# Up projection of a hybrid decoder block: a place in the ring and a pass order for each of twenty units, and a four-column fp32 product in every granule

## The chip, the cores and the metric

The kernel runs on one core of a Trainium2 chip. Its time is the device time of one execution in microseconds. TensorE (PE) multiplies, with weight loads (PEld) that can run ahead of the products; VectorE (DVE), ScalarE (ACT) and GpSimd (POOL) work beside it, and SyncE (SP) issues most transfers. Each engine works off its own queue in order.

## The reference

One decoder layer on x of 512 tokens by 2048 features, all in float32:

```python
def conv_ffn(h, w_ffn_in, conv_w, conv_b, w_ffn_out):
    S = h.shape[1]
    up = h @ w_ffn_in                       # 512 x 2048 by 2048 x 11264
    a, b = up[..., :D_FF], up[..., D_FF:]   # D_FF = 5632
    a_pad = jnp.pad(a, ((0, 0), (CONV_W - 1, 0), (0, 0)))
    a = (conv_w[0] * a_pad[:, 0:S] + conv_w[1] * a_pad[:, 1:S + 1]
         + conv_w[2] * a_pad[:, 2:S + 2] + conv_b)
    return (jax.nn.gelu(a, approximate=True) * b) @ w_ffn_out

def reference(x, ...):
    h = rmsnorm(x, attn_pre_norm)
    m = token_mixer(h, ...)       # gated linear attention and differential attention, then w_o
    x = x + rmsnorm(m, attn_post_norm)
    h = rmsnorm(x, ffn_pre_norm)
    f = conv_ffn(h, w_ffn_in, conv_w, conv_b, w_ffn_out)
    return x + rmsnorm(f, ffn_post_norm)
```

The change lies in the product `h @ w_ffn_in`, called the up projection.

## The kernel before

**Split products.** A float32 product is made from three products in the reduced format fp32r. Each operand v is split into a high half (v rounded to fp32r, by ACT, line 135) and a low half (v minus the high half, by DVE, line 136); then w·s is taken as high·high, high·low and low·high. The activations are split once and stay: `ah` and `al` hold them transposed. The weights come from memory in granules of 128 partitions by 1,024 values and are split on the way.

**The ring.** The two halves of a granule go to `ring`, one tile of 7 × 1,024 values for each partition. There are three slots for high halves (0, 1, 2) and three for low halves (3, 4, 5), and the seventh thousand is room behind them. `halves` steps the slot by one, modulo three, and returns the high and the low range; both are moved up by `place_w[0]` elements, which is the *place* of the weights. Before the change the place is 16 in the up projection's units and 0 everywhere else. One element has four bytes.

**Units.** After the first block of 512 columns, done plainly, the up projection is cut into 20 units: ten blocks of 512 columns for each of the two branches a and b of the reference. A unit multiplies in Strassen–Winograd form: seven products of blocks (`x0`, `z0`, `y0`, `z1`, `x1`, `y1`, `y2`) with the activation sums `a11`, `a12`, `a22`, `s5`, `s2`, `s3`, `s7`, and weight sums that are made in place, by accumulating transfers that POOL issues (line 873) and by DVE. `Unit.run` does one such product: two granules, each split by `granule` and multiplied by `up_prods`. There a granule is 4 rows of blocks (k) by 2 column blocks (n) by 3 passes, 24 products of a 128 × 128 weight block with 256 columns of activations (lines 924 to 926): the weights are the stationary operand, so that every product has its own weight load.

**Order.** The loop at the end of the functions shown runs one unit after the other, with the ends laced: `x0` of the next unit comes before `y2` of this one, and `z0` of the next after it. The down projection's units (`a` of 2, products of 512 columns, lines 1021 to 1023) follow in the same manner, the first one's `x0` before the last up unit's `y2`. Chains `x` and `z` accumulate in the PSUM pool `psm`, `y` in the pool `psa`, with four banks each. This stage is not in an order written by hand: the framework's planner orders each engine's instructions with a timeline of its own, and puts in the waits that overlapping reads and writes need.

Of the kernel before, what the change touches and what calls it, by code (L numbers as in the profile page):

```python
# [9 lines left out]
F32 = mybir.dt.float32  # L10
# [20 lines left out]
GR = 1024  # L31
# [4 lines left out]
def hybrid_layer(ctx: ExitStack, tc: tile.TileContext, x, attn_pre_norm, w_in, w_alpha_up, b_alpha,  # L36
# [19 lines left out]
    mm = nc.tensor.matmul  # L56
# [5 lines left out]
    psa = ctx.enter_context(tc.tile_pool(name="psa", bufs=4, space=PSUM))  # L62


    ident = few.tile([P, P], F32, name="ident")
# [11 lines left out]
    def bank(pool=None):  # L77
        return (pool or psa).tile([P, 512], F32, name="bank", tag="bank")
# [27 lines left out]
    place_w = [0]  # L106

    ring = wpool.tile([P, 7 * GR], F32R, name="ring", bufs=1)
    slot = [0]

    def halves():
        slot[0] = (slot[0] + 1) % 3
        return [ring[:, GR * i + place_w[0]:GR * (i + 1) + place_w[0]] for i in (slot[0], slot[0] + 3)]

    kept = []

# [9 lines left out]
    def granule(src, a, raw=None, spare=None, hl=None):  # L126
        if raw is None:
            raw = load(src, a)
        if hl is not None:
            hi, lo = hl[:, 0, :], hl[:, 1, :]  # L130
        elif spare:
            hi, lo = spare_halves(spare)
        else:
            hi, lo = halves()
        act(hi, raw, AF.Copy)  # L135
        tt(lo, raw, hi.bitcast(F32), ALU.subtract)  # L136
        r = "p (a b) -> p a b"
        return hi.rearrange(r, a=a), lo.rearrange(r, a=a)
# [8 lines left out]
    def split(hi, lo, src):  # L147
        act(hi, src, AF.Copy)  # L148
        tt(lo, src, hi.bitcast(F32), ALU.subtract)  # L149
# [485 lines left out]
    order = [(s + 8) % 16 for s in range(KT)]  # L635
# [129 lines left out]
    def pair_tile():  # L765
        return small_tile("u").rearrange("p (n t) -> p n t", n=2)


    def conv(c, b, f):
        act(c, b, AF.Identity, bias=conv_col(3, f), scale=conv_col(2, f))  # L770
        stt(c[:, 1:], b[:, :S - 1], conv_col(1, f), c[:, 1:], ALU.mult, ALU.add)
        stt(c[:, 2:], b[:, :S - 2], conv_col(0, f), c[:, 2:], ALU.mult, ALU.add)
        act(c, c, AF.Gelu_apprx_tanh)
# [27 lines left out]
    HK = KT // 2  # L801
# [50 lines left out]

    turn = [0]
    extra = [False]

    class Unit:
        def __init__(self, a, block, prods, chain, out):
# [3 lines left out]
        def run(self, seg, op, raws):  # L861
            c = seg[0]
            if seg[1] == "0":
                self.banks[c] = self.chain(c)
            for g in range(2):
                turn[0] += 1
                place_w[0] = 16 if self.a == 4 else 0
                hl = granule(None, self.a, raws[g], spare=extra[0] and turn[0] % 4 == 0)
                self.prods(self.banks[c], op, g, hl, seg[1] == "0")

# [42 lines left out]
    NOW = dict(skip_group_check=True)  # L913


    def up_prods(b, op, g, w, start):
        sh, sl = up[op]
        for n in range(2):
            o = b[:, 256 * n:256 * (n + 1)].rearrange("p (t c) -> p t c", c=P)
            for k in range(4):  # L920
                wh = w[0][:, k, n * P:(n + 1) * P]
                wl = w[1][:, k, n * P:(n + 1) * P]
                kk = 4 * g + k
                mm(o, wh, sh[:, :, kk, :], start=start and kk == 0 and n == 0, stop=False, **NOW)  # L924
                mm(o, wh, sl[:, :, kk, :], start=False, stop=False, **NOW)  # L925
                mm(o, wl, sh[:, :, kk, :], start=False, stop=kk == HK - 1, **NOW)  # L926

    held = {}

    def up_unit(gi, br):  # L930
        col0 = DFF * br + 512 * gi
        T = [slice(0, 256), slice(256, 512)]
        st = {}

        def block(i, j, g):
            return w_f3[:, HK * i + 4 * g:HK * i + 4 * g + 4, col0 + 256 * j:col0 + 256 * (j + 1)]

        def chain(c):
            return bank(psa if c == "y" else psm)

        def out(seg, b):
            v = b.rearrange("p (n t) -> p n t", n=2)
            if seg == "x0":
                st["p1"] = fp.tile([P, 2, 256], F32, name="p1", tag="p1", bufs=2)
                act(st["p1"], v, AF.Copy)
            elif seg == "z0":
                st["u1"] = pair_tile()
                tt(st["u1"][:, :, T[1]], v, st["p1"], ALU.subtract)
            elif seg == "y0":
                stt(st["u1"][:, :, T[0]], v, -1.0, st["p1"], ALU.mult, ALU.subtract)  # L950
            elif seg == "z1":
                tt(st["u1"][:, :, T[0]], st["u1"][:, :, T[0]], v, ALU.add)
            elif seg == "x1":
                st["u0"] = pair_tile()
                act(st["u0"][:, :, T[0]], v, AF.Copy)
            elif seg == "y1":
                tt(st["u1"][:, :, T[1]], st["u1"][:, :, T[1]], v, ALU.subtract)
                if br == 0:
                    activate(1)
                else:  # L960
                    product(1)
            elif seg == "y2":
                tt(st["u0"][:, :, T[1]], v, st["p1"], ALU.add)
                if br == 0:
                    activate(0)
                else:
                    product(0)
                    token_sums(gi, st["u0"], st["u1"])

        def activate(j):  # L970
            c = held[gi, j] = pair_tile()
            for n in range(2):
                conv(c[:, n, :], st[f"u{j}"][:, n, :], 4 * gi + 2 * j + n)

        def product(j):
            u = st[f"u{j}"]
            tt(u, u, held.pop((gi, j)), ALU.mult)

        return Unit(4, block, up_prods, chain, out)


    def token_sums(gi, u0, u1):
        c, i = (gi - 1) // 2, (gi - 1) % 2
        T = [slice(0, 256), slice(256, 512)]
        a11, a21, a12, a22 = u0[:, :, T[0]], u0[:, :, T[1]], u1[:, :, T[0]], u1[:, :, T[1]]

        def put(n, src):
            dma(sd[c][n][:, i, :].rearrange("p (n t) -> p n t", n=2), src)

        def add(n, x, y, op):  # L990
            t = fp.tile([P, 2, 256], F32, name=n, tag="sum", bufs=2)
            tt(t, x, y, op)
            put(n, t)
            return t

        put("a11", a11)
        put("a12", a12)
        put("a22", a22)
        s5 = add("s5", a21, a22, ALU.subtract)
        s2 = add("s2", s5, a11, ALU.subtract)  # L1000
        add("s7", a11, a21, ALU.subtract)
        add("s3", s2, a12, ALU.add)
# [4 lines left out]
    def piece(v, t, h):  # L1007
        return v[:, t, HK * h:HK * (h + 1), :].rearrange("p k c -> p (k c)")

    def prepare(c, n):  # L1010
        raw = small_tile("st")
        dma(raw, sd[c][n].rearrange("p g x -> p (g x)"))
        split(piece(ah, *place[n]), piece(al, *place[n]), raw)
# [17 lines left out]
    def down_unit(c, cb):  # L1031
# [17 lines left out]

        return Unit(2, block, down_prods, chain, out)  # L1050

    ups = [up_unit(gi, br) for gi in range(1, NG) for br in range(2)]
    for i, u in enumerate(ups):
        nxt = ups[i + 1] if i + 1 < len(ups) else None
        if i == 0:
            u.x0()
            u.z0()
        u.y0()
        u.z1()
        if i == 0:  # L1060
            for h, r in enumerate(s7raw):
                split(up["s7"][0][:, h], up["s7"][1][:, h], r)
        if nxt is None:
            prepare(0, "a11")
        u.x1()
        if nxt is None:
            prepare(0, "s5")
        u.y1()
        if nxt is not None:
            nxt.x0()  # L1070
            u.y2()
            nxt.z0()
        else:
            downs = [down_unit(c, cb) for c in range(NG // 2) for cb in range(2)]
            downs[0].x0()
            prepare(0, "s2")
            u.y2()
# [125 lines left out]
    for q, at in enumerate(((3, 1), (0, 0))):  # L1203
        raw = small_tile("st")
        dma(raw, ud0[:, 2 * q:2 * q + 2, :].rearrange("p n t -> p (n t)"))
        hi, lo = (piece(v, *at) for v in (ah, al))
# [34 lines left out]
```

## Time and profile before

| what | us |
|---|---|
| two runs | 2150.64 and 2164.94, median 2157.79 |
| span of the profiled execution | 2150.8 |
| PE busy | 2112.4 |
| DVE busy | 1414.6 |
| ACT busy | 898.3 |
| up projection's units, first to last product | 928 to 1706 |

The profiled execution's own time is not given apart from its span; the span agrees with the lower of the two runs to 0.2 us. Where a start is given it counts from the first instruction. The duration of a product in the trace (276 ns for 256 columns) has the time through the array in it, and products overlap: how fast they follow each other is seen from their starts, or from how many lie in a stretch of time. A plain fp32 product shows as two instructions, each with a weight load; an fp32r product or a transpose shows as one.

### The profile page before, as it was taken

The page shows a single profiled execution, that of the slowest core. Times are in us where ns is not written, and L with a number is a line of the kernel's source. Part 1 is how long each engine was busy: PE and PEld are TensorE (multiplying, and loading weights), DVE is VectorE, ACT ScalarE, POOL GpSimd, SP SyncE. Part 2 cuts the span into 40 slices and gives each one's busy share as a digit, 9 for nine tenths or more (in the row PEclk, how much of TensorE's full clock was granted, in tenths as well). Part 3 has the DMA queues.
Part 4 walks back from the last instruction along what each step waited for, and adds up shares of the span by engine and source line. Part 5 has one row for each costly group of instructions (what it writes and reads, how often), then busy time and mean ns, then how long its engine had stood idle before and what let it go on. Part 6 is the DMA issues. An engine that isn't in the chain of part 4 may idle for free.

```text
span 2150.8 us, 31861 instructions
## 1 busy us (share of the span) xinstructions
PE 2112.4 (98%) x13009; PEld 1875.4 (87%) x13009; DVE 1414.6 (66%) x1725; ACT 898.3 (42%) x1162; POOL 199.2 (9%) x242
## 2 busy tenths in 40 slices
PE   7999999999999999999999999999999899999998
PEld 6878888888888889999999999999999778787786
DVE  5345554443444237688777786777778777888887
ACT  4233332333343224344544553544454554443433
POOL 1000000000000001011111111111110111110100
PEclk9999999999999999999999999999999999999999
DMA  6322222223224335455776757667577777676653
GB/s 214 99 75 79 79 69 79 79 79 88 78 80 169 95 128 186 128 119 136 172 172 149 175 139 189 149 157 191 129 172 177 203 229 182 171 195 170 158 167 145
DMA packets 218471, 303.83 MB, mean 141 GB/s; under 512 B 11776, under 2 KB 155572, under 8 KB 216404
## 3 DMA queue, kind: packets, MB, share of 16 engines
q1 hardware_dynamic: 165204, 238.87, 33.4%
q0 software_dynamic: 53120, 62.92, 19.1%
q8 instruction: 102, 1.67, 0.3%
q14 instruction: 45, 0.37, 0.1%
HBM read 273.97 MB, written 27.79 MB: 140 GB/s over the span
## 4 chain that ended last, share of the span: by engine, by line
PE 46%; issue 45%; POOL 4%; DVE 3%; DMA 2%; ACT 1%; POOLq 0%; SPq 0%; DVEq 0%; ACTq 0%
PE bank L189 7%; PE bank L190 7%; PE bank L191 7%; PE bank L173 5%; PE bank L171 5%; PE bank L172 5%; POOL rt L873 2%; PE bank L926 2%; PE bank L925 2%; PE bank L924 2%; POOL raw L873 2%; PE bank L439 1%; PE bank L507 1%; PE bank L538 1%; DVE ring L136 1%
## 5 line engine op out<-in xcount | busy, mean ns | idle before, releaser
L136 DVE TENSOR_TENSOR ring<-raw,ring 128x1024 fp32r<-128x1024 f32 x305 | 371.6, 1221 | 353.8 <-ACT ring L135 344.1
L135 ACT ACTIVATE ring<-raw 128x1024 fp32r<-128x1024 f32 x305 | 323.1, 1060 | 596.6 <-PE bank L191 157.3
L926 PE MATMUL bank<-ah,ring 128*128 128x256 f32 x1280 | 353.7, 276 | 0.8 <-DVE ring L136 0.8
L924 PE MATMUL bank<-ah,ring 128*128 128x256 f32 x1280 | 353.5, 276 | 0.0
L925 PE MATMUL bank<-al,ring 128*128 128x256 f32 x1280 | 353.4, 276 | 0.0
L136 DVE TENSOR_TENSOR ring<-rt,ring 128x1024 fp32r<-128x1024 f32 x221 | 269.0, 1220 | 89.8 <-ACT ring L135 87.9
L135 ACT ACTIVATE ring<-rt 128x1024 fp32r<-128x1024 f32 x221 | 233.1, 1060 | 223.5 <-PE bank L925 146.1
L926 PEld LDWEIGHTS bank<-ah,ring 128*128 128x128 f32 x1280 | 240.3, 188 | 1.2 <-DVE ring L136 1.2
L925 PEld LDWEIGHTS bank<-al,ring 128*128 128x128 f32 x1280 | 240.4, 188 | 0.1
L924 PEld LDWEIGHTS bank<-ah,ring 128*128 128x128 f32 x1280 | 240.3, 188 | 0.1
L189 PE MATMUL bank<-ring,ah 128*128 128x512 f32 x600 | 236.9, 398 | 0.8 <-ACT ah L148 0.8
L190 PE MATMUL bank<-ring,ah 128*128 128x512 f32 x600 | 235.8, 394 | 0.0
L191 PE MATMUL bank<-ring,al 128*128 128x512 f32 x600 | 235.0, 394 | 0.0
L171 PE MATMUL bank<-ah,ring 128*128 128x512 f32 (+1 forms) x512 | 196.2, 383 | 0.0
L173 PE MATMUL bank<-ah,ring 128*128 128x512 f32 (+1 forms) x512 | 194.7, 380 | 0.0
L172 PE MATMUL bank<-al,ring 128*128 128x512 f32 (+1 forms) x512 | 194.5, 380 | 0.0
L1022 PE MATMUL bank<-ring,ah 128*128 128x512 f32 x424 | 166.7, 393 | 7.3 <-DVE ring L136 7.2
L1023 PE MATMUL bank<-ring,al 128*128 128x512 f32 x424 | 165.8, 391 | 0.0
L1021 PE MATMUL bank<-ring,ah 128*128 128x512 f32 x424 | 158.8, 393 | 3.2 <-ACT ring L135 2.4
L191 PEld LDWEIGHTS bank<-ring,al 128*128 128x128 f32 x600 | 113.2, 189 | 24.3 <-DVE al L149 0.3
L189 PEld LDWEIGHTS bank<-ring,ah 128*128 128x128 f32 x600 | 113.1, 189 | 24.2 <-ACT ah L148 1.2
L190 PEld LDWEIGHTS bank<-ring,ah 128*128 128x128 f32 x600 | 113.3, 189 | 23.7 <-DVE ring L136 0.5
(260 smaller groups left out, 4063.6 us busy)
## 6 DMA issues: line engine op xcount, KB each, us to landing
raw<-in_w_in_dram SPq DMA_DIRECT2D x96, 512.0 KB, 3.7
raw<-in_w_ffn_in_dram SPq DMA_DIRECT2D x96, 512.0 KB, 5.1
raw<-in_w_ffn_out_dram SPq DMA_DIRECT2D x48, 512.0 KB, 7.3
rt<-in_w_ffn_in_dram SPq DMA_DIRECT2D x40, 512.0 KB, 6.6
rt<-in_w_ffn_in_dram POOLq DMA_DIRECT2D x40, 512.0 KB, 6.2
raw<-in_w_ffn_in_dram POOLq DMA_DIRECT2D x40, 512.0 KB, 6.8
raw<-in_w_o_dram SPq DMA_DIRECT2D x32, 512.0 KB, 3.7
rt<-in_w_ffn_out_dram SPq DMA_DIRECT2D x20, 512.0 KB, 8.1
```

Source lines behind the costliest of these rows:

```text
L135: act(hi, raw, AF.Copy)
L136: tt(lo, raw, hi.bitcast(F32), ALU.subtract)
L171: mm(o, wh, ah[:, t0:t1, kk, :], start=st, stop=False)
L172: mm(o, wh, al[:, t0:t1, kk, :], start=False, stop=False)
L173: mm(o, wl, ah[:, t0:t1, kk, :], start=False, stop=sp)
L189: mm(banks[t], ah[:, t, s, :], w[0][:, k, :], start=st, stop=False)
L190: mm(banks[t], ah[:, t, s, :], w[1][:, k, :], start=False, stop=False)
L191: mm(banks[t], al[:, t, s, :], w[0][:, k, :], start=False, stop=sp)
L924: mm(o, wh, sh[:, :, kk, :], start=start and kk == 0 and n == 0, stop=False, **NOW)
L925: mm(o, wh, sl[:, :, kk, :], start=False, stop=False, **NOW)
L926: mm(o, wl, sh[:, :, kk, :], start=False, stop=kk == HK - 1, **NOW)
L1022: mm(b[j], sh[:, o:o + P], w[1][:, q, :], start=False, stop=False, **NOW)
```

## The change

Each of the 20 units gets a place for its high halves, a place for its low halves, and an order of the three passes: 0 is (high, high), (high, low), (low, high), as before, and 1 is (high, high), (low, high), (high, low). Units of the down projection keep place 0. In every granule of an up unit, ahead of the first product of the second column block, there is one small product in plain fp32: the identity matrix as weights, four columns of the low half as the moving operand, into a PSUM bank of its own, `nudge`, that nothing reads.

```diff
     def halves():
         slot[0] = (slot[0] + 1) % 3
-        return [ring[:, GR * i + place_w[0]:GR * (i + 1) + place_w[0]] for i in (slot[0], slot[0] + 3)]
+        return [ring[:, GR * i + p:GR * (i + 1) + p] for i, p in ((slot[0], place_w[0]), (slot[0] + 3, place_w[-1]))]
...
             for g in range(2):
                 turn[0] += 1
-                place_w[0] = 16 if self.a == 4 else 0
+                place_w[:] = self.places if self.a == 4 else (0,)
+                order[0] = self.order if self.a == 4 else 0
                 hl = granule(None, self.a, raws[g], spare=extra[0] and turn[0] % 4 == 0)
...
                 kk = 4 * g + k
-                mm(o, wh, sh[:, :, kk, :], start=start and kk == 0 and n == 0, stop=False, **NOW)
-                mm(o, wh, sl[:, :, kk, :], start=False, stop=False, **NOW)
-                mm(o, wl, sh[:, :, kk, :], start=False, stop=kk == HK - 1, **NOW)
+                if n == 1 and k == 0:
+                    mm(nudge[0][:, 0:4], ident, wl.bitcast(F32)[:, 0:4], start=True, stop=True, **NOW)
+                passes = [(wh, sh), (wh, sl), (wl, sh)] if order[0] == 0 else [(wh, sh), (wl, sh), (wh, sl)]
+                for i, (w1, s1) in enumerate(passes):
+                    mm(o, w1, s1[:, :, kk, :], start=start and kk == 0 and n == 0 and i == 0,
+                       stop=kk == HK - 1 and i == 2, **NOW)
...
+    nudge = [bank(psa)]
     ups = [up_unit(gi, br) for gi in range(1, NG) for br in range(2)]
+    RELATIONS = [(16, 16, 0), (80, 80, 0), (12, 12, 0), (20, 20, 0), (14, 14, 0), (18, 18, 0), (16, 80, 0), (80, 16, 0),
+                 (16, 0, 0), (16, 32, 0), (16, 16, 1), (80, 80, 1), (12, 12, 1), (20, 20, 1), (16, 48, 1), (88, 88, 0),
+                 (72, 72, 0), (0, 16, 1), (16, 0, 1), (16, 112, 0)]
+    for u, (hi, lo, o) in zip(ups, RELATIONS):
+        u.places, u.order = (hi, lo), o
```

More of the change, by code (lines that the diff above doesn't have):

```diff
@@ L854, in hybrid_layer @@
     extra = [False]
+    order = [0]
     class Unit:
```

## The prediction

> **What bounds the kernel now.** I read the page first, then the table by stage, then the waits inside the up projection, then the order of time around its end.
>
> ```profile
> span 2150.8 us, 31861 instructions
> PE 2112.4 (98%) x13009; PEld 1875.4 (87%) x13009; DVE 1414.6 (66%) x1725; ACT 898.3 (42%) x1162; POOL 199.2 (9%) x242
> PEclk9999999999999999999999999999999999999999
> ```
>
> TensorE is busy 98% of the span at full granted clock; DVE has a third of the span free. Whatever the change adds to the stream of products comes out at the end, unless it fits into a gap, and there are hardly any. Waits of PE, then of ACT, from 925 to 1688 us:
>
> ```profile
> PE bank L926 <- DVE ring L136: 1.8, 4, 0.6
> ACT ring L135 <- PE bank L925: 256.5, 186, 2.8
> ```
>
> In 763 us PE lost 1.8 us to a late split. ACT's waits (total, times, longest) say how the stage runs: the high half of a granule goes into the ring as soon as L925, the last reader of a high half, is done with the slot. That release is for the granule three before, so the split has two granules of PE time in hand. Note that L925 ends it and not L926, which reads only the low half: reuse of the ring is followed by address range within the tile.
>
> How fast PE goes is in the table by stretches (us, PE busy and instructions, PEld, DVE, ACT, POOL, clock, DMA share, GB/s):
>
> ```profile
> 854.00:884.00 30.00, 30.00 (x252) 30.00 (x251) 8.77 (x10) 5.30 (x6) 0.00 (x0) 1.00 0.42 131
> 930.00:940.00 10.00, 10.00 (x87) 10.00 (x86) 9.83 (x9) 5.29 (x7) 0.00 (x0) 1.00 0.33 85
> 950.00:1130.00 180.00, 180.00 (x1591) 180.00 (x1590) 136.44 (x140) 87.31 (x97) 22.90 (x18) 1.00 0.69 164
> 1140.00:1340.00 200.00, 200.00 (x1767) 200.00 (x1766) 150.63 (x153) 91.66 (x99) 26.08 (x21) 1.00 0.72 171
> ```
>
> All four hold products of 256 columns with nothing missing; a count includes up to two products cut by the window's ends. The first (weights at place 0, or in spare tiles) gives 30/250 = 120 ns for a product. The other three have place 16: 10/85 = 118 ns before a short wait near 943 us, and 180/1589 = 113.3 ns after it. So the pace depends on where the weights lie, and at one place it has at least two values, with a short break between them. The change touches just that.
>
> **The parts of the change.** There are 20 units of 7 products of blocks, with 2 granules each: 280 granules of 24 products, 6,720 in all (2,240 of each of the three lines).
>
> ```profile
> L924 PE MATMUL bank<-ah,ring 128*128 128x256 f32 x1280 | 353.5, 276 | 0.0
> L924 PE MATMUL bank<-s3h,ring 128*128 128x256 f32 x320 | 88.4, 276 | 0.0
> ```
>
> (s5h and s2h have 320 each as well.)
>
> *The small product.* 280 times, identity as fp32 weights, four fp32 columns. No fp32 product in the trace is that narrow; the nearest are the 64-column ones of L439:
>
> ```profile
> 160.72 0.39 PE L191 MATMUL bank<-ring,al 128*128 128x512 f32 x1
> 160.94 1.00 PE L439 MATMUL bank<-qe,d 128*128 128x64 f32 x8
> 161.75 0.48 PE L189 MATMUL bank<-ring,ah 128*128 128x512 f32 x1
> 162.07 0.33 PE L439 MATMUL bank<-qe,d 128*128 128x64 f32 x2
> 160.72 1.08 PEld L439 LDWEIGHTS bank<-qe,d 128*128 128x128 f32 x8
> 161.72 0.19 PEld L189 LDWEIGHTS bank<-ring,ah 128*128 128x128 f32 x1
> 161.84 0.54 PEld L439 LDWEIGHTS bank<-qe,d 128*128 128x128 f32 x3
> ```
>
> The source makes four products there and the trace has eight, each with its own load: an fp32 product is two passes. From 160.72 to 162.07 are 1.35 us; the two 512-column products take 0.227 each, so eight passes cost 0.896, or 0.112 each. The loads say why: one follows the other by (161.72 − 160.72 − 0.227)/7 = 0.11 us, though 64 columns would stream sooner. Narrower columns therefore save nothing: two passes, 2 × 0.112 = 0.224 us, and nothing hides them, since the load after the second pass has only four columns to hide under. 280 × 0.224 = **62.7 us**. The low end is from the transposes:
>
> ```profile
> L439 PEld LDWEIGHTS bank<-qe,d x224: 187/192/193, 160.7 to 343.4; 128*128 128x128 f32 x112
> L156 PEld LDWEIGHTS bank<-ident,xt x64: 138/140/230, 9.8 to 51.7; 128*128 128x128 f32 x64
> ```
>
> If loads of this product were as short as those around the identity (140 against 192 ns), a pass would cost 0.060 and all of it 34 us. L439 is nearer, being a plain product, so I take 62.7. A gain from the extra work itself is excluded: PE has no idle time that it could fill. It adds no wait (its operands were waited for by the first half of the granule), and its PSUM bank leaves three for the one `y` chain that a unit holds.
>
> *The places and the ring.* Slots are 1,024 elements apart with no room between, so when the place falls from one granule to the next, the new granule's first elements lie on the last ones of the granule just before, which PE reads last. The split must then wait for the previous granule instead of the third before. Units interleave at their ends (`x0` of the next, `y2` of this one, `z0` of the next), so a change of place is crossed two or three times. I went through the 280 granules with the 20 relations, the slots turning by three from the slot that the overlaps of before imply (another start gives 16 and 26, or 20 and 22, in place of the counts below). With high place above low place, as in (80, 16) and twice (16, 0), a high half in slot 2 also overlaps the low half of slot 0, in every third granule of the unit. Counted: 16 granules whose high half waits for the granule before, 27 whose low half alone does; before the change, 1 and 1, both where the place goes from 16 to 0 at the end of the stage. (Overlaps the other way meet only the first 128 elements of a granule two before, which PE has left by then: nothing.) The first of the two in order of time, PE, then ACT and DVE:
>
> ```profile
> 1705.49 0.28 PE L925 MATMUL bank<-al,ring 128*128 128x256 f32 x1
> 1705.61 0.28 PE L926 MATMUL bank<-ah,ring 128*128 128x256 f32 x1
> 1706.92 0.73 PE L1021 MATMUL bank<-ring,ah 128*128 128x512 f32 x2 [1.03 <-ACT ring L135]
> 1708.35 0.50 PE L1022 MATMUL bank<-ring,ah 128*128 128x512 f32 x1 [0.69 <-DVE ring L136]
> 1708.68 0.40 PE L1023 MATMUL bank<-ring,al 128*128 128x512 f32 x1
> 1708.92 0.40 PE L1021 MATMUL bank<-ring,ah 128*128 128x512 f32 x1
> 1705.81 1.06 ACT L135 ACTIVATE ring<-rt 128x1024 fp32r<-128x1024 f32 x1 [1.77 <-PE bank L925]
> 1707.08 1.21 DVE L136 TENSOR_TENSOR ring<-rt,ring 128x1024 fp32r<-128x1024 f32 x1
> ```
>
> Unhindered, L1021 would start at 1705.73 and the product now at 1708.92 four times 0.227 later, at 1706.64: 2.3 us lost. A low half alone: free 0.04 after L926's end at 1705.89 (as ACT after L925), DVE 1.22, PE 0.06 later at 1707.21, where the third product of an up granule was due at 1705.96, and 0.10 for a load that could not run ahead: 1.35 us. 15 × 2.3 + 26 × 1.35 = 34.5 + 35.1 = **69.6 us**. No cover exists: the wait is for PE's own last product, and both products of a granule pair go to the same bank. Behind the waiting split on DVE's queue stand the evacuations and weight sums, a third of DVE's time being free for them.
>
> *The pace.* Twenty relations, one of which (16, 16, first order) is the old one, each re-entered after 280 breaks. Bounds: 113.3 − 0.112 × 1000 = 1.3 ns less, −9 us, if every product ran at the load cadence; 120 ns, +45 us, if all ran as at place 0. The old place shows both 113 and 118 and the other place 120, so I take the middle, 116.6: 6,720 × 3.3 = **+22 us**.
>
> Sum: 62.7 + 69.6 + 22 = 154. The profiled execution spans 2150.8, as the lower run (2150.64); the median 2157.79 lies 7 above. 2157.8 + 154 = **2312**.
>
> **Rivals.** (1) *Small products nearly free.* At 34 us the time is 2283. The Trainium skill (TensorE: Matmul & The Clock Gate, Back-to-back issue gap) gives 1 to 64 columns a floor of about 25 ns; by that, 560 passes would be 14 us and the sum 2264. The 0.112 of L439's 64 columns disagrees. (2) *Splits queued badly.* The other of the two old overlaps, ACT, DVE, then PE:
>
> ```profile
> 1682.69 1.06 ACT L135 ACTIVATE ring<-rt 128x1024 fp32r<-128x1024 f32 x1 [1.66 <-PE bank L925]
> 1690.91 1.22 DVE L149 TENSOR_TENSOR al<-st,ah 128x1024 fp32r<-128x1024 f32 x1 [3.18 <-ACT ah L148]
> 1692.05 1.22 DVE L136 TENSOR_TENSOR ring<-rt,ring 128x1024 fp32r<-128x1024 f32 x1
> 1693.33 0.50 PE L1022 MATMUL bank<-ring,ah 128*128 128x512 f32 x1 [4.65 <-DVE ring L136]
> ```
>
> Here the planner put a split of reloaded sums ahead of the blocked low half on DVE, and that one waited for its load: 4.65 us instead of 1.35. If half of the 26 went so, 13 × 3.3 = 43 more, 2355; all, 2398. Against it: such reloads come at the end of the stage only. (3) *A better state.* The small product sets the stream to a faster pace. At the load cadence of 112 ns the pace term is −9 instead of +22: 2281. For "no change" it must give back all but 43 of the 132 us of the other terms: 13.3 ns a product, so 100 ns decides; at 97 ns the time is 2157.8 + 132.3 − 109.5 = 2181. For it: the pace has states, and transposes load faster. Against: the load cadence of 112 ns. The Trainium skill (TensorE: Matmul & The Clock Gate, Back-to-back issue gap) has N/2.4 + 2.5, which is an estimate of 109 ns for 256 columns, a pace term of −28 and 2262; no stretch quoted here shows it. (4) *The places cause no waits* (the overlaps are not followed as I read them): 2157.8 + 62.7 + 22 = 2242.
>
> **How the numbers follow.** Forecast 0.60; rival 1 0.11; rival 2 0.15; rival 3 0.10, of which 0.04 under 100 ns; rival 4 0.04. 2% (43 us) is about what a measurement of this kernel tells from no change. Faster 0.01, same 0.04, slower 0.95. The range takes in pace ends of the forecast (2281 to 2335), rival 1 below its 2283 by a faster pace, and rival 2 to beyond half: 2250 to 2370.
>
> **What would show it.** The new line's products: 560 in the profile, each granule's first half to its second 0.22 longer. ACT's high-half splits released by the granule just before, 16 times, and DVE's low halves 27 more. PE's idle time in the stage: from 2 to some 60 us, at unit ends and inside the eighth, ninth and nineteenth units. In windows between breaks: 113 to 120 ns, differing by unit. I am wrong if the small product shows one pass, if idle time stays at a few us, or if a unit runs well off 113 to 120.

## The result, and the profile after

The changed kernel takes 2339.55 us (median of 2 runs, 2335.15 to 2343.95) against 2157.79: a ratio of 1.0837, with a 95% interval of 1.0736 to 1.0937. It is slower, as forecast; 2312 was predicted, 27.5 us too little, and the range, 2250 to 2370, holds the time. The profiled execution took 2335.15, its span is 2333.4, so 1.7 us lie around the span.

The page of the changed kernel, to be held against the lines of before:

```profile
span 2333.4 us, 32952 instructions
PE 2238.3 (96%) x13569; PEld 1993.6 (85%) x13569; DVE 1422.6 (61%) x1725; ACT 903.0 (39%) x1162; POOL 199.5 (9%) x242
```

PE has 560 instructions more, all from the small products; DVE, ACT and POOL do what they did. Of the 182.6 us added to the span 126 are busy PE time, and PE's share falls from 98% to 96%, so there is new idle time as well. The stage itself, from the first up product to the last, in the table by stretches (us, PE, PEld, DVE, ACT, POOL, clock, DMA share, GB/s), before and after:

```profile
928.00:1705.70 777.70, 771.21 (x6745) 768.40 (x6743) 597.82 (x607) 376.14 (x411) 101.70 (x80) 1.00 0.69 163
```

```profile
928.00:1891.00 963.00, 898.88 (x7295) 885.62 (x7294) 603.62 (x607) 378.36 (x411) 101.70 (x80) 0.97 0.57 131
```

Two things stand in the second row that the first has not: 64 us in which PE is not busy (6.5 before), and a granted clock of 0.97. The waits of PE in this stage of the changed kernel (total us, times, longest):

```profile
PE bank L930 <- DVE ring L136: 40.9, 35, 2.2
PE bank L930 <- ACT ring L135: 19.9, 20, 1.2
```

Before it was 1.8 us, from 925 to 1688. The products of all three passes now have one line, L930; the small product's is L927.

From the starts of the products in the two traces I summed the stage product by product, from the first up product to the start of the product after the last one: 766.9 us before, 954.8 after, 188 more. (The rest of the kernel is 5 us shorter, most of it in shorter waits of the down projection behind the stage.) By parts:

| term | forecast | measured |
|---|---|---|
| small products, 280 | 62.7 | 63 (0.225 each) |
| waits at the ring, at full clock | 69.6 | 72.5 |
| pace of the products | 22 | 25 |
| halved clock behind waits | not in it | about 27 (the rest); some 25 read off the starts |

### The profile page after: what moved, and what is told of

It reads as the page before. It is cut to its first block, busy times and chain, and to the rows that moved or that the text cites. A ratio compares the mean times of both kernels' runs of the same rounds, so it can differ in the third digit from the quotient of the medians.

```text
span 2333.4 us, 32952 instructions
## 1 busy us (share of the span) xinstructions
PE 2238.3 (96%) x13569; PEld 1993.6 (85%) x13569; DVE 1422.6 (61%) x1725; ACT 903.0 (39%) x1162; POOL 199.5 (9%) x242
## 4 chain that ended last, share of the span: by engine, by line
PE 55%; issue 36%; DVE 3%; POOL 2%; DMA 2%; ACT 1%; SPq 0%; POOLq 0%; DVEq 0%; ACTq 0%
PE bank L930 15%; PE bank L189 6%; PE bank L190 6%; PE bank L191 6%; PE bank L173 5%; PE bank L171 5%; PE bank L172 5%; DVE ring L136 2%; POOL rt L875 1%; POOL raw L875 1%; PE bank L439 1%; PE bank L507 1%; PE bank L538 1%; PE bank L927 1%; PE bank L156 1%
## 5 line engine op out<-in xcount | busy, mean ns | idle before, releaser
L930 PE MATMUL bank<-ah,ring 128*128 128x256 f32 x2560 | 506.2, 292 | 37.6 <-DVE ring L136 25.6
L930 PEld LDWEIGHTS bank<-ah,ring 128*128 128x128 f32 x2560 | 412.8, 194 | 44.8 <-DVE ring L136 30.3
L930 PE MATMUL bank<-al,ring 128*128 128x256 f32 x1280 | 364.8, 285 | 0.0
L930 PEld LDWEIGHTS bank<-al,ring 128*128 128x128 f32 x1280 | 248.2, 194 | 0.1
L930 PE MATMUL bank<-s5h,ring 128*128 128x256 f32 x640 | 132.7, 299 | 19.9 <-DVE ring L136 11.9
L189 PEld LDWEIGHTS bank<-ring,ah 128*128 128x128 f32 x600 | 112.9, 188 | 23.7 <-ACT ah L148 0.8
L930 PE MATMUL bank<-s2h,ring 128*128 128x256 f32 x640 | 125.0, 288 | 2.1 <-DVE ring L136 2.1
```

Of the source, the lines that this page charges most:

```text
L189: mm(banks[t], ah[:, t, s, :], w[0][:, k, :], start=st, stop=False)
L930: mm(o, w1, s1[:, :, kk, :], start=start and kk == 0 and n == 0 and i == 0, stop=kk == HK - 1 and i == 2, **NOW)
```

## The experiments

**Small products alone.** Every unit gets the old relation, and the small products stay.

```diff
-    RELATIONS = [(16, 16, 0), (80, 80, 0), ...]
+    RELATIONS = [(16, 16, 0)] * 20
```

> All units at (16, 16), first order, with the small products: no granule gets a new overlap. Theory (small product 0.225 us each; each of them breaks the stream, and after it the pace is about 118 ns instead of 113): 63 us for the small products, some 28 us of pace, no new waits, no halved clock: span about 2150.8 + 91 = 2242. Rival A (the slower pace comes from the places, not from the breaks): pace stays at 113, span about 2214. Rival B (the halved clock comes from the small products): windows of halved clock remain and the span goes over 2260.

The span is 2236.4 (2237.6 us, 1.0345 of before, interval 1.0159 to 1.0531). Up products that follow each other with no wait or small product between are on average 117.8 ns apart in every unit but the first and the last (117.6). The places are those of before, so the slower pace comes from the breaks: rival A fell. Rival B fell too: two windows of halved clock are left, one at the end of the stage, where the place still goes from 16 to 0, and one behind it. The changed kernel's order of time shows one break (PE, then the loads):

```profile
1010.05 0.28 PE L930 MATMUL bank<-al,ring 128*128 128x256 f32 x1
1010.17 0.28 PE L930 MATMUL bank<-ah,ring 128*128 128x256 f32 x1
1010.28 0.28 PE L927 MATMUL bank<-ring,ident 128*128 128x4 f32 x2
1010.42 0.36 PE L930 MATMUL bank<-ah,ring 128*128 128x256 f32 x1
1010.62 0.28 PE L930 MATMUL bank<-al,ring 128*128 128x256 f32 x1
1010.74 0.40 PE L930 MATMUL bank<-ah,ring 128*128 128x256 f32 x2
```

```profile
1010.17 0.30 PEld L927 LDWEIGHTS bank<-ring,ident 128*128 128x128 f32 x2
1010.39 0.19 PEld L930 LDWEIGHTS bank<-ah,ring 128*128 128x128 f32 x1
1010.51 0.19 PEld L930 LDWEIGHTS bank<-al,ring 128*128 128x128 f32 x1
1010.63 0.30 PEld L930 LDWEIGHTS bank<-ah,ring 128*128 128x128 f32 x2
```

The last product ahead starts at 1010.17, the second one behind at 1010.62. Two steps of 0.118 were due, 0.45 were taken, so some 0.22 were lost (0.456 less 0.236 by the nanosecond): the first load of the pair hides under the product ahead, and the two after it, the pair's second and that of the next product, are exposed.

**A wider small product.**

```diff
-                    mm(nudge[0][:, 0:4], ident, wl.bitcast(F32)[:, 0:4], ...)
+                    mm(nudge[0][:, 0:64], ident, wl.bitcast(F32)[:, 0:64], ...)
```

> As with all units at (16, 16) and all small products, but each small product is 64 columns wide instead of 4. Theory (a pass is bound by its weight load, 0.112 us, under which 64 columns still hide): the same span to 2 us, 2236. Rival (the pass is paid by its columns on top of the load): the columns add 60 x 2 x 0.42 ns = 50 ns a product, 14 us in all, span about 2250.

Span 2235.2 (one run) against 2236.4 with four columns: sixteen times the columns cost nothing. What is paid is two weight loads.

**The relations alone.** The small products and their bank are taken out.

```diff
-                if n == 1 and k == 0:
-                    mm(nudge[0][:, 0:4], ident, ...)
...
-    nudge = [bank(psa)]
```

> The twenty relations without the small products, ring as in the change. Theory: waits of some 70 us and 20 to 28 us of halved clock behind them, as in the changed kernel; between waits most units near 113 ns, since a wait lets the stream settle there: span about 2150.8 + 95 = 2246. Rival A (places set the pace): the units differ as in the changed kernel, 115 to 119 ns, and the span is about 2270. Rival B (the halved clock needs the small products): no halved windows in this stage, span about 2220.

The span is 2285.1 (2281.7 us, 1.0549 of before, interval 1.0351 to 1.0746), 39 more than the theory gave. Waits there are and halved windows too, so rival B fell, but two parts were larger. The waits came to 90 us (by the starts, less the 4.4 of before) instead of 70:

```profile
PE bank L928 <- DVE ring L136: 54.1, 42, 4.3
PE bank L928 <- ACT ring L135: 22.3, 20, 2.3
```

And the pace did not settle at 113 between the waits: it cost 24 us, as in the changed kernel. There rival A had it right for most relations; the two runs that follow separate it.

**The ring spread out.** The slots' starts are 1,152 elements apart. Six slots fit in the seven thousand of the tile, and places up to 112 can no longer make two slots meet. First with the whole change:

```diff
-        return [ring[:, GR * i + p:GR * (i + 1) + p] for i, p in ...]
+        at = GR + 128
+        return [ring[:, at * i + p:at * i + GR + p] for i, p in ...]
```

> The changed kernel with the ring's slots 1,152 elements apart instead of 1,024, so that no relation makes two granules overlap. Theory: waits (some 72 us) and the halved clock behind them (some 25) go, small products (63) and the pace (25) stay: span about 2333 - 97 = 2236. Rival (the waits have another cause, such as the planner's order or one PSUM bank less): PE's idle time stays, span over 2300.

Span 2232.1 (2233.6 us, 1.0326 of before, interval 1.0141 to 1.0512). PE's waits in the stage, then the stage's row:

```profile
PE bank L931 <- DVE ring L137: 1.1, 1, 1.1
```

```profile
928.00:1784.00 856.00, 854.89 (x7262) 853.73 (x7262) 599.95 (x601) 375.20 (x408) 101.62 (x80) 1.00 0.62 146
```

The waits are gone, the clock is back at 1.00, and 101 us of span with them, where I had put 97. So the waits are overlaps of neighbours in the ring, as counted, and the halved clock hangs on the waits. The small products and the pace are left.

**Relations on the spread ring, without small products.**

> The twenty relations with the spaced ring and without the small products: neither breaks nor waits. Theory (the pace is a state that breaks decide, and places only decide which state a break leads to): long stretches at one pace, most at 113, some units perhaps at 118 to 120 from their start on; span 2145 to 2170. Rival (every relation has its own pace): the units differ from one to the next as in the changed kernel, span about 2150.8 - 8 + 25 = 2168 or more.

Span 2159.6 (2163 us, 1.0023 of before, interval 0.9964 to 1.0081). Now hardly anything breaks the stream within a unit (three waits of 0.5 to 1.1 us are left, in the seventh, eighth and last), and the mean step between products of each unit can be read from the starts:

| relation (high, low, order) | ns |
|---|---|
| (16, 80, 0), (16, 112, 0), (16, 16, 1), (80, 80, 1), (16, 48, 1) | 113.3 to 113.6 |
| (80, 16, 0) | 116.2 (113.3 up to the wait at 1218.1, 117.8 behind it) |
| (16, 16, 0), (80, 80, 0), (14, 14, 0), (16, 0, 0), (12, 12, 1), (0, 16, 1), (16, 0, 1) | 117.8 |
| (18, 18, 0), (16, 32, 0), (72, 72, 0) | 118.2 to 118.4 |
| (20, 20, 0), (20, 20, 1), (12, 12, 0) | 118.8 to 119.0 |
| (88, 88, 0) | 120.0 |

Theory and rival each have a part. A place that is off the multiples of 16 has a pace of its own, 117.8 to 120, with or without breaks. But (16, 16, 0), which ran at 113.3 before the change for nearly the whole stage, stays at 117.8 here for a whole unit: it has two paces, and which one it keeps hangs on what came before it. It is not alone. In the run with the relations alone (80, 80, 0) ran at 113.3, and (16, 16, 1) and nearly all of (80, 80, 1) at 117.8, each the other way round from this table. So the table gives the pace that each relation had in this run, and for these not the only one.

**One break in each unit.** Old relation, old ring.

```diff
-                if n == 1 and k == 0:
+                if n == 1 and k == 0 and op == "a11" and g == 1:
```

> All units at (16, 16), first order, with one small product in each unit instead of fourteen (the second granule of x0), ring as before. Theory (113 and 118 ns are lasting states, and a break picks one): 20 x 0.225 = 4.5 us of small products, and after the first of them the pace is 118 ns for most of the stage, until a wait resets it: 20 to 28 us of pace, span 2175 to 2185. Rival (the slower pace is a transient of a dozen products after each break): 4.5 us and 2 us of pace, span about 2157.

Span 2171.5 in the profiled execution, the shortest of eight; the median is 2178.6 us, 1.0088 of before, interval 1.0040 to 1.0136. A stretch between two breaks:

```profile
1140.00:1180.00 40.00, 40.00 (x342) 40.00 (x341) 28.75 (x28) 16.04 (x17) 5.08 (x4) 1.00 0.66 158
```

340 products in 40 us are 117.6 ns. From the second unit on, one small product and the 335 products after it run slow: the pace is lasting, not a transient. 20 breaks cost nearly as much pace (28 us) as 280 do. The first small product alone was undone: behind a product that came 0.04 us late, at 942.1, the stream went to 113.3 until the next small product.

**All units at (16, 112), with all small products.**

> All units at (16, 112), first order, with all 280 small products. Theory (after a break the relation decides to which state the stream returns, and this one returns to 113 ns): 63 us of small products, about 4 us of pace, no overlaps between granules: span about 2218. Rival (any break leads to 118): as with (16, 16), span about 2237.

Span 2213.4 (2214.9 us, 1.0278 of before, interval 1.0181 to 1.0375). The mean step is 113.9 ns in all units, with 117.8 at (16, 16): this relation comes back to the fast pace within a few products after each break. The same 40 us with all small products, (16, 16) first:

```profile
1140.00:1180.00 40.00, 40.00 (x343) 40.00 (x342) 27.67 (x28) 17.61 (x20) 5.08 (x4) 1.00 0.52 117
```

```profile
1140.00:1180.00 40.00, 40.00 (x354) 40.00 (x353) 27.47 (x28) 18.14 (x20) 5.08 (x4) 1.00 0.63 145
```

Of 86 us that the small products add at (16, 16), 23 are pace and are avoided by moving the low halves by 96 elements.

**The kernel before on a spread ring, and (16, 112) on it, without small products.**

```diff
-    RELATIONS = [(16, 16, 0), (80, 80, 0), ...]
+    RELATIONS = [(16, 112, 0)] * 20
```

> The kernel before with nothing but the ring's slots 1,152 elements apart. It has two overlaps of places, at the end of the stage, and they go. Theory: some 8 us less there (5.0 and 2.3 us of waits and one halved window), the rest as before, if a wait still brings the stream from 118 to 113 early in the stage: 2143. If the planner's order leaves no such wait, the stage stays at 118 ns: up to 30 us more, 2172. Rival (the waits at the end come from the reloads, not from the overlap): within 2 us of 2151.

> All units at (16, 112), first order, slots 1,152 apart, no small products. Theory (this relation returns to 113 ns by itself, whatever the break): 113.4 ns from the first unit on, some 2 us saved in the first granules, and the waits at the end of the stage gone: span about 2142, faster than the kernel before by 0.3 to 0.5%. Rival (113 there came from the neighbours' state): some units at 118, span 2150 to 2175.

The same stretch of both, the old place first:

```profile
1140.00:1180.00 40.00, 40.00 (x342) 40.00 (x341) 28.98 (x28) 16.27 (x17) 5.08 (x4) 1.00 0.66 158
```

```profile
1140.00:1180.00 40.00, 40.00 (x355) 40.00 (x354) 29.36 (x30) 16.94 (x17) 5.08 (x4) 1.00 0.75 180
```

That is 340 products and 117.6 ns against 353 products and 113.3 ns. At the old place nothing brought the stream out of the slow pace: it entered the stage in it, there was no wait, and it stayed for all 6,720 products; 2168.05 us, 1.0056 of before, interval 1.0021 to 1.0090, although its waits were gone. With (16, 112) the time is 2142.10 us, 0.9932 of before, interval 0.9898 to 0.9966: less than both kernels of this case take, by a margin over before that is clear of the interval and below the 2% that count as faster.

**(16, 112) on the old ring.** What of that is place, and what is ring?

> All units at (16, 112), first order, no small products, slots 1,024 apart as before. Theory (the gain of (16, 112) with spaced slots has two parts, a pace that always returns to 113 ns and the missing waits at the stage's end): the pace part stays, 113.3 ns in every run of it, and the waits at the end of the stage come back, 5 to 9 us: span about 2145, times in one group. Rival (the spacing alone made the pace): units at 118 ns, span over 2165.

2146.12 us, 0.9933 of before, interval 0.9896 to 0.9970, span 2144.6; 113.3 ns in the units. The place is most of it; the spread ring adds some 4 us (2142.10 against 2146.12, on two chips). In the runs beside this kernel the one before ranges from 2142.64 to 2174.99, and this one from 2141.43 to 2149.67. So the shortest times of the two are alike, and what (16, 112) lacks is the long ones. That the kernel before keeps the slow pace in some of its runs would explain its spread, but none of its long runs was profiled, so this is argued and not shown.

## Why the prediction was right

*The small product.* Right in number and reason: 280 small products of two passes, 0.225 us each, bound by loads; the wide one settles it. Rival 1 with 0.06 a pass, and the 25 ns floor of the Trainium skill (TensorE: Matmul & The Clock Gate, Back-to-back issue gap) are excluded for this product: with its own load ahead of each pass the four columns pay 112. (By that floor the prediction's sum is 2263, not 2264.)

*The ring.* Right to the granule. Put on granules by the starts of the products, 75.2 us of loss fall on the 41 granules that the count had named for this stage (15 by their high half, 26 by their low half alone; the two at the stage's end, which were there before, are left out) and less than 0.5 us on the other 239. By kind the prices were 2.3 and 1.35 us; measured are 2.68 and 1.35 in the mean. (The 72.5 of the table is the whole stage less the 4.4 us that before had.) Single waits differ, from 0 to 3.3 us, since some splits stood behind other work. The wait at 1100.6, ACT and then DVE:

```profile
1100.79 1.06 ACT L135 ACTIVATE ring<-rt 128x1024 fp32r<-128x1024 f32 x1 [2.00 <-PE bank L930]
1100.90 0.69 DVE L962 TENSOR_TENSOR u<-u,bank 128x512 f32<-128x512 f32 x1 [0.86 <-PE bank L930]
1101.63 1.22 DVE L982 TENSOR_TENSOR u<-u 128x1024 f32<-128x1024 f32 x1
1102.77 1.22 DVE L136 TENSOR_TENSOR ring<-rt,ring 128x1024 fp32r<-128x1024 f32 x1
```

The high half was ready at 1101.85, the low half's split began at 1102.77, behind an evacuation's sum and the product of the two branches. So rival 2 happened in small, with work that was ready and not with reloads. With the relations alone the same 41 granules lost 86.3 us, up to 4.45 in one, and others 7: the places of the waits are sure, their lengths are good to some 20 us.

*The pace.* The size was right, 25 for 22, and the bounds 113 to 120 held in all twenty units. The reason was half there, and the size in part luck. I took the middle between two places for want of better. In fact there are two causes, and either alone costs about as much as both: the relations without small products lose 24 us, on the old ring and on the spread one alike, and the small products at the old place break the fast pace for good and lose 28.

*The missing term.* The term that was mis-sized is "15 × 2.3 + 26 × 1.35 = 34.5 + 35.1": it prices the waits and not what they do to the clock. The row for it was there in the stretch behind the first overlap of before:

```profile
1688.30:1712.00 23.70, 17.33 (x90) 14.34 (x89) 19.16 (x18) 11.73 (x13) 3.28 (x3) 0.93 0.82 201
```

A clock of 0.93 over 23.7 us is one window of 3.4 us at half speed, behind the wait of 4.65 us; the page's clock line, in tenths, reads 9 all along and hides it. Five windows of the changed kernel, each 3.41 us long:

```profile
1059.63:1063.05 3.42, 1.64 (x11) 1.22 (x10) 1.23 (x1) 2.09 (x3) 0.00 (x0) 1.00 0.54 153
1063.05:1066.46 3.41, 3.41 (x18) 3.41 (x17) 2.45 (x2) 0.51 (x1) 0.00 (x0) 0.50 0.51 154
1155.20:1158.61 3.41, 3.17 (x27) 2.96 (x26) 2.58 (x4) 2.43 (x4) 0.00 (x0) 1.00 0.84 132
1158.61:1162.03 3.42, 1.89 (x14) 1.67 (x14) 1.48 (x2) 2.28 (x3) 0.00 (x0) 1.00 0.57 166
1162.03:1165.44 3.41, 3.41 (x31) 3.41 (x30) 2.42 (x3) 1.06 (x1) 0.00 (x0) 1.00 0.43 141
```

In the first window PE waits twice, with 1.31 and 1.03 us from start to start, and the whole next one runs at a clock of 0.50, 18 products instead of 31. At 1158 it waits just as long, 1.31 and 1.04, but the first of these waits began in the window before, and nothing happens. The changed kernel has 17 halved windows in this stage, 58 us. In them the products start 0.213 us apart in the median, where 0.118 is usual; by the starts the windows cost some 25 us, which is about what the sum lacks. The spread ring takes them away together with the waits.

## What to carry to other kernels

Count a wait of PE twice: once for itself, and, when it empties most of a clock window, once for the half clock behind it. A change of offset within a ring of slots without room between is also a change of who waits for whom, and 128 spare elements between slots undo it. Where a stream of products is as tight as its weight loads, look at the steps between starts before and after a break: an offset that returns to the fast pace by itself is worth more than one that is fast when undisturbed.

## What the runs showed of the hardware

*Two lasting paces.* At (16, 16) the 256-column products follow each other every 113.3 or every 117.8 ns, for hundreds of products, until something breaks the stream. There 278 of 280 small products left it at 117.8, and the waits for a late split that the kernel before had left it at 113.3. That is no rule for other relations: at (80, 16) on the spread ring a wait of 1.1 us took the stream from 113.3 to 117.8. (16, 112) returns to 113.3 after either kind of break. (16, 80), too, runs at 113.3 undisturbed, but with the small products of the changed kernel its unit had 117.7. Why 96 elements between the halves do this was not found.

*The clock's windows.* The halved windows of a run all lie on one grid of 3.413 us. I added up, for each window of that grid in five runs, the time in which no product was streaming (256 columns taken as 113 ns from a start): all 33 windows at full clock in which that was 2.057 us or more were followed by a halved one, and none below 2.01 was; the five between are mixed. In all twelve runs of this case it is 37 of 37, and still none below 2.01. The Trainium skill (TensorE: Matmul & The Clock Gate, What's actually happening) puts the half clock after at least one idle window of about 3.4 us. Here PE need not be idle for a whole window: about 60% of one is enough, and a loss of 2.1 us in two waits halves the clock or not by where it falls.
